# A hybrid decoder step: five page buffers instead of four, nineteen operand buffers instead of eighteen, and a quarter of the dynamic DMA scratch

## The chip, the cores and the metric

The kernel runs on one core of one Trainium2 chip. The metric is the device time of one execution in microseconds (us), as the median of several runs. All data and all results are 32-bit floats.

## What is computed

The reference is one inference step of a decoder layer (DEPTH 1) for two groups of rows that share the weights: a prompt of 1024 rows of width 1024, and 8 sample rows, each with a paged cache of 8192 past positions (64 pages of 128 positions, 8 heads of 64, looked up through a page table). Cut to what matters:

```python
def fox_attend(q, k, v, cq, ck, qpos, kpos):
    s = jnp.einsum('bqhd,bkhd->bhqk', q, k) * (ATT_HEAD_DIM ** -0.5)
    s = s + (cq.transpose(0, 2, 1)[:, :, :, None] - ck.transpose(0, 2, 1)[:, :, None, :])
    s = jnp.where(kpos[None, :] <= qpos[:, None], s, -jnp.inf)
    p = jax.nn.softmax(s, axis=-1)
    return jnp.einsum('bhqk,bkhd->bqhd', p, v)

# the prompt; the samples do the same with k, v, logf of the cache in front of their own
q, k, v, logf, u, z = mixer_inputs(rmsnorm(xp, g_mix), w_in, b_f, g_sgu_v)
xp = xp + merge_heads(fox_prompt(q, k, v, logf), sgu_prompt(u, z, w_s, b_s), g_att_out, g_sgu_out, w_o)
mk, mv = memory_kv(mem_prompt, g_mem, w_ck, w_cv)             # 256 memory rows, 4 heads of 256
xp = xp + cross_attend(rmsnorm(xp, g_cross), mk, mv, w_cq, w_co)
f, conv_p = conv_ffn(rmsnorm(xp, g_ffn), 0, w_up, conv_w, conv_b, w_down)   # width 2 x 2816, silu gate
xp = xp + f
y_prompt = rmsnorm(xp, g_final)
```

`cq` and `ck` are the running sums of the log forget gates. Besides both groups' outputs the new keys, values, gates and states are returned.

## The kernel before

Two streams of work are emitted together. The **main stream** is the prompt, in two halves of 512 rows: projections, attention with spatial gating beside it, the output projection, cross-attention, the gated feed-forward and the final norm. Each large product is made on TensorE (PE) from three matmuls (`gemm3`, L272 to L274) of weights and operands that ScalarE (ACT, L235) and VectorE (DVE, L236, L239) split into a high and a low part. Weight blocks are loaded on SP's queue into `wr`; operands lie in tiles of 128 x 1024, called `u`.

The **sample stream** is the generator `decode`, and after it `sample_rest`. For each of the 8 samples it takes 16 K pages and 16 V pages, each of 128 x 2048 floats, one step at a time. `kstep` (L1428) gathers a K page into a `kv` tile by an indirect DMA that GpSimd (POOL) issues; DVE multiplies it in place with the query and sums over each head into the scores `s` (L1444 and L1448, or in four quarter steps L1435 and L1436 while the main stream is in its attention). `vstep` (L1489) gathers a V page likewise, and 16 narrow matmuls on PE (L1495) add its share to `dv`. Two pages of K and two of V alternate in the order of allocation. After `decode`, the same tiles carry the samples' weights (L1568), and at the start of the kernel they carry the prompt's rows and the sample rows.

In the attention, PE makes a block of scores (L807 to L811), DVE its row maximum (`mx`, L813 and L816), ACT the exponentials (L814, L817); PE turns these (L836), ACT or DVE copies them (L841, L843), and PE multiplies them with V (L852). In the output projections a row factor `fac` is made by ACT (L1031) and a power on POOL (L1032). In the cross-attention ACT copies the turned weights (L1208) before the product at L1216.

A table `PACE` sets how often the sample stream takes a step beside the main stream. This sets the order in which the instructions are written; the page's DVE and PE work is pinned behind the newest instruction of the main stream on that engine (`behind`). Then the framework's scheduler sorts each engine's instructions anew, by its own model of times in which buffers that are in use hold work back. So the number of buffers changes the order on every engine.

The tiles come from rotating pools. A new tile takes the oldest buffer of its kind and waits until that buffer's last reader is done:

```python
def U(shape, dt=F32):
    ...
    t = upool.tile([P, UW], dt, tag="u", bufs=NU, name=nm("u"))[:, :n]
    ...
def KV():
    return dpool.tile([P, 2048], F32, tag="kv", bufs=NKV, name=nm("kv"))
```

Constants lie in on-chip memory behind a scratch area that the program reserves for the dynamic DMAs of GpSimd, by default 16384 bytes on each partition; the pools follow.

Of the kernel before, what the change touches and what calls it, by code (L numbers as in the profile page):

```python
# [47 lines left out]

NKV = 4
VLAG = 2
MIXR = 1.0
G0R = 0.0
# [9 lines left out]
M3 = 3  # L64
MB = 0
BR = 3
NU = 18
NT = 7
HP = 1
SD = 1  # L70
# [8 lines left out]
def build(nc, tc, ctx, a, phases=None):  # L79
# [27 lines left out]
    def nm(s):  # L107
        cnt[0] += 1
        return f"{s}_{cnt[0]}"

    def U(shape, dt=F32):
        n = 1
        for s in shape[1:]:
            n *= s
        t = upool.tile([P, UW], dt, tag="u", bufs=NU, name=nm("u"))[:, :n]
        if len(shape) == 3:
# [6 lines left out]
    def KV():  # L123
        return dpool.tile([P, 2048], F32, tag="kv", bufs=NKV, name=nm("kv"))

# [1909 lines left out]
```

## Time and profile before

| what | us |
|---|---|
| runs | 1790.96, 1792.46, 1794.57 |
| median | 1792.46 |
| profiled execution, span (the page gives no other time of its own) | 1791.7 |
| PE busy | 1735.9 |
| DVE busy | 1399.9 |
| ACT busy | 733.5 |
| POOL busy | 488.3 |

The profile shows one execution. PE, DVE, ACT and POOL are the engines named above, PEld the loading of weights into PE, SP the queue that issues most plain DMAs. A row such as `kv<-cache_k,io` names the tile written and the tensors read; `dv` and `s` are the sample attention's sums and scores. A wait `A x L1 <- B y L2` means that engine A stood before line L1 until B's work at L2 was done. A bracket behind a row is the engine's idle time before it and what ended it. The stages lie, in us from the span's start, roughly so: projections to 315, attention 315 to 500 (the rest of it and the gating after that), first output projection and cross-attention to 715, first feed-forward to 1110, the second half's merge from there, its output projection and cross-attention 1170 to 1345, its feed-forward and the samples' rest to 1779, and the last norm.

### The profile page before, as it was taken

What the parts mean: (1) busy time and instruction counts of PE and PEld (TensorE: products, weight loads), DVE (VectorE), ACT (ScalarE), POOL (GpSimd) and SP (SyncE); (2) the same over time, 40 slices, a digit from 0 to 9 for tenths busy, and PEclk for the clock granted to TensorE, in tenths of its full rate; (3) what the DMA queues carried; (4) which work ended last, traced back from release to release, by engine and by line L of the source; (5) the groups of instructions that cost most, each with busy time, mean ns of one, the idle gap of its engine ahead of it and who ended that gap; (6) DMA issues with size and microseconds to landing.
All of it is one profiled execution on the core that took longest, in us unless ns stands there. A gap on an engine that the chain in (4) does not pass through costs nothing.

```text
span 1791.7 us, 25124 instructions
## 1 busy us (share of the span) xinstructions
PE 1735.9 (97%) x9653; PEld 1285.7 (72%) x9653; DVE 1399.9 (78%) x1733; ACT 733.5 (41%) x1374; POOL 488.3 (27%) x461
## 2 busy tenths in 40 slices
PE   8999999889999999999999999999999999999997
PEld 5787777655677666767777777766666778768875
DVE  4689658989788986989999999898885549855344
ACT  6332355566643635333333244335353233333232
POOL 1252234443222332333322223433322112102110
PEclk9999999999999999999999999999999999999999
DMA  8786798777697975779788788988879587568982
GB/s 291 297 304 226 294 334 319 259 264 244 254 403 279 363 299 224 282 285 345 290 301 313 291 317 311 376 306 346 320 280 350 214 306 249 191 260 297 359 310 80
DMA packets 157074, 521.06 MB, mean 291 GB/s; under 512 B 20874, under 2 KB 40842, under 8 KB 124186
## 3 DMA queue, kind: packets, MB, share of 16 engines
q0 software_dynamic: 57168, 341.14, 50.0%
q1 hardware_dynamic: 92874, 165.73, 26.5%
q10 hardware_dynamic: 6912, 12.59, 1.9%
q8 instruction: 76, 1.25, 0.3%
q14 instruction: 44, 0.36, 0.1%
HBM read 495.47 MB, written 23.93 MB: 290 GB/s over the span
## 4 chain that ended last, share of the span: by engine, by line
PE 53%; issue 9%; DMA 8%; DVE 6%; ACT 2%; POOL 2%; POOLq 0%; DVEq 0%; ACTq 0%; SPq 0%
DMA kv<-cache_v,io 6%; PE ba L272 6%; PE ba L274 6%; PE ba L273 6%; PE dv L1495 4%; PE bb L272 3%; PE bb L273 3%; PE bb L274 3%; PE ba L1063 1%; DVE s L1448 1%; PE ba L1064 1%; PE ba L1065 1%; PE dv L331 1%; DMA kv<-cache_k,io 1%; PE dv L1774 1%
## 5 line engine op out<-in xcount | busy, mean ns | idle before, releaser
L235 ACT ACTIVATE wh<-wr 128x1024 fp32r<-128x1024 f32 (+2 forms) x220 | 228.6, 1044 | 443.3 <-PE ba L273 142.3
L236 DVE TENSOR_TENSOR wl<-wr,wh 128x1024 fp32r<-128x1024 f32 (+2 forms) x220 | 262.7, 1200 | 165.1 <-PE ba L274 57.4
L1428 POOL DMA_INDIRECT kv<-cache_k,io x128 | 186.9, 1460 | 606.8 <-DVE s L1448 327.2
L1444 DVE TENSOR_TENSOR kv<-kv,d 128x1024 f32<-128x1024 f32 (+1 forms) x156 | 258.0, 1681 | 32.6 <-DMA kv<-cache_k,io 32.6
L1448 DVE TENSOR_REDUCE s<-kv 128x16 f32<-128x1024 f32 (+1 forms) x156 | 258.4, 1672 | 0.0
L1489 POOL DMA_INDIRECT kv<-cache_v,io x128 | 160.8, 1256 | 239.4 <-PE dv L1495 155.2
L272 PE MATMUL ba<-u,wh 128*128 128x512 f32 x528 | 209.3, 397 | 0.0
L274 PE MATMUL ba<-u,wl 128*128 128x512 f32 x528 | 209.0, 396 | 0.0
L273 PE MATMUL ba<-u,wh 128*128 128x512 f32 x528 | 208.5, 395 | 0.5 <-DVE u L239 0.5
L272 PE MATMUL ba<-wh,u 128*128 128x512 f32 (+1 forms) x495 | 186.1, 379 | 0.9 <-ACT u L235 0.9
L273 PE MATMUL ba<-wl,u 128*128 128x512 f32 (+1 forms) x495 | 185.1, 375 | 1.3 <-DVE wl L236 1.3
L274 PE MATMUL ba<-wh,u 128*128 128x512 f32 (+1 forms) x495 | 183.4, 375 | 0.0
L1495 PE MATMUL dv<-kv,s 128*32 128x512 f32 x1024 | 127.1, 598 | 1.6 <-DMA kv<-cache_v,io 1.6
L274 PEld LDWEIGHTS ba<-u,wl 128*128 128x128 f32 x528 | 99.2, 188 | 29.0 <-issue 6.5
L272 PEld LDWEIGHTS ba<-u,wh 128*128 128x128 f32 x528 | 99.3, 188 | 26.4 <-issue 4.8
L273 PEld LDWEIGHTS ba<-u,wh 128*128 128x128 f32 x528 | 99.2, 188 | 25.2 <-issue 2.3
L272 PEld LDWEIGHTS ba<-wh,u 128*128 128x128 f32 x495 | 93.0, 188 | 25.0 <-issue 6.5
L272 PE MATMUL bb<-u,wh 128*128 128x512 f32 x272 | 108.7, 400 | 0.0
L274 PE MATMUL bb<-u,wl 128*128 128x512 f32 x272 | 108.0, 398 | 0.0
L273 PE MATMUL bb<-u,wh 128*128 128x512 f32 x272 | 107.9, 397 | 0.0
L273 PEld LDWEIGHTS ba<-wl,u 128*128 128x128 f32 x495 | 93.0, 188 | 20.1 <-DVE wl L236 1.9
L274 PEld LDWEIGHTS ba<-wh,u 128*128 128x128 f32 x495 | 92.9, 188 | 19.5 <-issue 1.6
(454 smaller groups left out, 3310.6 us busy)
## 6 DMA issues: line engine op xcount, KB each, us to landing
wr<-w_up SPq DMA_DIRECT2D x88, 512.0 KB
kv<-w_up POOLq DMA_DIRECT2D x22, 1024.0 KB
wr<-w_down SPq DMA_DIRECT2D x40, 512.0 KB
kv<-w_down POOLq DMA_DIRECT2D x11, 1024.0 KB
wr<-w_in SPq DMA_DIRECT2D x16, 512.0 KB
wr<-w_o SPq DMA_DIRECT2D x16, 512.0 KB
wr<-w_cq SPq DMA_DIRECT2D x16, 512.0 KB
wr<-w_co SPq DMA_DIRECT2D x16, 512.0 KB
```

Source lines behind the costliest of these rows:

```text
L235: nc.scalar.activation(h, src, AF.Copy)
L236: nc.vector.tensor_tensor(l, src, h.bitcast(F32), op=ALU.subtract)
L272: mmul(out, sh, mh, start=(i == 0), stop=False)
L273: mmul(out, sh, ml, start=False, stop=False)
L274: mmul(out, sl, mh, start=False, stop=(i == n - 1))
L331: mmul(ps[32 * j : 32 * j + 32, :w], xT[:, k, :] if nk == 8 else xT[:, k * 8 : k * 8 + 32], raw[:, q, j * w : (j + 1) * w], start=(k == 0) ...
L1063: mmul(pss[i], mh[k][:, tb], wh, start=(k == korder[0]), stop=False)
L1428: nc.gpsimd.indirect_dma_start(kv, None, a["cache_k"], off(kidx[:, b, ch : ch + 1]))
L1444: nc.vector.tensor_tensor(kvv[:, i : i + m, :], kvv[:, i : i + m, :], qb.unsqueeze(1).broadcast_to((P, m, 512)), op=ALU.mult)
L1448: nc.vector.tensor_reduce(s[:, ch * 4 + i : ch * 4 + i + m, :].rearrange("p k h -> p (k h)"), kvv[:, i : i + m, :].rearrange("p k (h d) -> ...
L1489: nc.gpsimd.indirect_dma_start(kv, None, a["cache_v"], off(kidx[:, b, ch : ch + 1]))
L1495: mmul(dv[32 * j : 32 * j + 32, :], s[:, ch * 4 : ch * 4 + 4, :].rearrange("p k h -> p (k h)"), kvv[:, j, :], start=(ch == 1), stop=(ch == ...
```

## The change

Three numbers change. The dynamic scratch takes 4096 bytes on each partition instead of 16384, which frees 12,288. A fifth `kv` buffer takes 8192 of these and a nineteenth `u` buffer 4096.

```diff
-NKV = 4
+NKV = 5
...
-NU = 18
+NU = 19
...
-    nc = bacc.Bacc("TRN2", target_bir_lowering=False, num_devices=1)
+    nc = bacc.Bacc("TRN2", target_bir_lowering=False, num_devices=1, dynamic_dma_scratch_size=4096)
```

No instruction is added or removed on any engine; the order changes. Lines of difference between the orders before and after: PE 3002, DVE 1300, ACT 746, POOL 300, SP 168.

The first place is POOL's queue in the first feed-forward, about 750 to 780 us in the profile. The rows are page gathers; `kv_6843` and `kv_6844` are the V pages that the matmuls at 782 us read. In brackets stand the semaphores that a gather waits for (DMASW for an earlier page's landing, DVE or PE for the last reader of the buffer). Before:

```order
L1428 DMA kv_6751<-cache_k,io 128x2048 [waits DMASW6_49,DVE_49]
L1428 DMA kv_6839<-cache_k,io 128x2048 [waits DMASW7_49,DVE_49]
L1489 DMA kv_6844<-cache_v,io 128x2048 [waits DMASW2_49,PE_49]
L1489 DMA kv_6843<-cache_v,io 128x2048 [waits DMASW0_49,PE_49]
L1428 DMA kv_6883<-cache_k,io 128x2048 [waits DMASW3_49,DVE_49]
L1428 DMA kv_6973<-cache_k,io 128x2048 [waits DMASW6_49,PE_49]
```

The same six gathers after the change:

```order
L1428 DMA kv_6751<-cache_k,io 128x2048 [waits DMASW3_49,DVE_49]
L1428 DMA kv_6839<-cache_k,io 128x2048 [waits DMASW6_49,DVE_49]
L1489 DMA kv_6844<-cache_v,io 128x2048 [waits DMASW7_49,DVE_49]
L1489 DMA kv_6843<-cache_v,io 128x2048 [waits DMASW3_49,DVE_49]
L1428 DMA kv_6883<-cache_k,io 128x2048 [waits DMASW1_49,PE_49]
L1428 DMA kv_6973<-cache_k,io 128x2048 [waits DMASW0_49,PE_49]
```

The gathers keep their order here; what moved is the buffer that each one takes. The two V pages took the buffers of two earlier V pages, which PE reads, and now take those of K pages, which DVE reads.

The second place is DVE's order in the attention's second half. `d` is the query of a sample, L1435 and L1436 are quarter steps of a K page, `mx` a row maximum, `rl` and `u` belong to the main stream.

```order
 L1435 TENSOR_TENSOR kv_3757<-kv_3757,d_490_2860 128x512
 L863 RECIPROCAL rl_3957<-ls_3732 128x4
+L1435 TENSOR_TENSOR kv_3917<-kv_3917,d_490_2860 128x512
+L1436 TENSOR_REDUCE s_2862<-kv_3757 128x8
+L816 TENSOR_REDUCE mx_3896<-ba_3897 128x1
+L1436 TENSOR_REDUCE s_2862<-kv_3757 128x8
 L816 TENSOR_REDUCE mx_3933<-ba_3934 128x1
-L1436 TENSOR_REDUCE s_2862<-kv_3757 128x8
-L1435 TENSOR_TENSOR kv_3917<-kv_3917,d_490_2860 128x512
-L816 TENSOR_REDUCE mx_3973<-ba_3974 128x1
-L1436 TENSOR_REDUCE s_2862<-kv_3757 128x8
 L1436 TENSOR_REDUCE s_2862<-kv_3917 128x8
```

A product and two sums of pages that stood behind the maximum `mx_3933` stand ahead of it now, and `mx_3896`, made earlier before, stands among them. Over the whole attention 48 such quarter rows stood directly ahead of a maximum before, and 59 after.

The third place is POOL's queue around the row factors of the output projection that ends the second half's cross-attention, about 1316 us. `fac_2060`, `fac_2070`, `fac_2074` are three of its four factors, the other rows are V pages.

```order
 L1489 DMA kv_10835<-cache_v,io 128x2048
+L1489 DMA kv_10985<-cache_v,io 128x2048
+L1489 DMA kv_10984<-cache_v,io 128x2048
 L1032 TENSOR_TENSOR fac_2060_10931<-fac_2060_10931,mhalf 128x1
-L1489 DMA kv_10985<-cache_v,io 128x2048
+L1489 DMA kv_11203<-cache_v,io 128x2048
 L1032 TENSOR_TENSOR fac_2070_11012<-fac_2070_11012,mhalf 128x1
-L1489 DMA kv_10984<-cache_v,io 128x2048
-L1489 DMA kv_11203<-cache_v,io 128x2048
 L1489 DMA kv_11204<-cache_v,io 128x2048
+L1489 DMA kv_11253<-cache_v,io 128x2048
 L1032 TENSOR_TENSOR fac_2074_11023<-fac_2074_11023,mhalf 128x1
```

Two pages moved ahead of the first factor and a third, `kv_11203`, ahead of the second.

## The prediction

> **What bounds the kernel now.** I read the page's engine shares first, then the busy times in stretches, then the waits of all engines, then the timelines of the few PE rows that wait for work made from cache pages.
>
> ```profile
> span 1791.7 us, 25124 instructions
> PE 1735.9 (97%) x9653; PEld 1285.7 (72%) x9653; DVE 1399.9 (78%) x1733; ACT 733.5 (41%) x1374; POOL 488.3 (27%) x461
> ...
> q0 software_dynamic: 57168, 341.14, 50.0%
> ```
>
> PE is busy for 1735.9 of 1791.7 us, so no edit that leaves its matmuls alone can gain more than the 55.8 us in which it is idle, plus what the clock takes. The stretches tell where those 55.8 lie (stretch, length, busy time of PE, PEld, DVE, ACT, POOL, granted clock, DMA share, GB/s):
>
> ```profile
> 0.00:30.00 30.00, 22.85 (x92) 14.74 (x93) 16.38 (x45) 16.31 (x23) 0.98 (x6) 1.00 0.72 235
> 30.00:60.00 30.00, 29.57 (x143) 22.84 (x142) 4.92 (x10) 14.93 (x26) 10.15 (x10) 1.00 0.99 397
> 60.00:75.00 15.00, 12.57 (x103) 11.25 (x98) 12.11 (x7) 9.29 (x13) 0.00 (x0) 1.00 0.78 278
> 315.00:500.00 185.00, 165.27 (x1109) 115.66 (x1109) 162.26 (x287) 113.04 (x251) 63.60 (x82) 0.96 0.76 260
> 575.00:715.00 140.00, 134.43 (x669) 96.60 (x671) 114.64 (x144) 66.46 (x156) 40.24 (x35) 0.99 0.78 304
> 715.00:1110.00 395.00, 393.69 (x1859) 293.49 (x1852) 372.04 (x344) 141.91 (x220) 113.70 (x82) 1.00 0.81 302
> 1170.00:1345.00 175.00, 167.22 (x868) 117.83 (x867) 151.01 (x181) 78.83 (x174) 58.16 (x50) 1.00 0.83 313
> 1779.00:1792.00 13.00, 3.40 (x15) 2.44 (x13) 5.68 (x10) 1.45 (x4) 1.58 (x3) 0.73 0.40 161
> ```
>
> Length less PE busy gives 10.0 us in the first 75 us, 19.7 in the attention (315 to 500), 5.6 and 7.8 in the two middles (output projection and cross-attention), 1.3 in the whole first feed-forward, 9.6 behind the last matmuls. The attention is the only long stretch with a granted clock clearly below 1. There, as at 699.6, the rate falls to half for stretches of 3.4 us; the stretches at 317.3, 354.8, 368.5 (two in a row) and 699.6 make 17.0 us at half rate, of which these are the first and the last:
>
> ```profile
> 317.30:320.70 3.40, 2.98 (x16) 2.27 (x16) 3.31 (x6) 0.62 (x3) 0.60 (x1) 0.50 1.05 408
> ...
> 699.60:703.00 3.40, 3.40 (x18) 3.40 (x17) 2.27 (x7) 0.58 (x2) 1.01 (x1) 0.50 0.64 266
> ```
>
> One such stretch with PE busy costs about half of 3.4, 1.7 us.
>
> Now the page buffers. The waits of all engines (total, times, longest):
>
> ```profile
> POOL kv L1428 <- DVE s L1448: 327.2, 68, 28.2
> POOL kv L1489 <- PE dv L1495: 155.2, 41, 11.4
> POOL kv L1428 <- PE dv L1495: 127.5, 18, 14.7
> ...
> DVE kv L1444 <- DMA kv<-cache_k,io: 32.6, 18, 5.6
> ```
>
> POOL issues the page gathers and waits over 600 us for one of the four buffers. That is idle time of an engine with 27% work and costs nothing by itself. What counts is whether DVE (for K) and PE (for V) meet a page that has not landed. DVE does so 18 times, 32.6 us in all. On PE I followed every idle gap back to its releaser; these five end at a page (start, length, row, idle before):
>
> ```profile
> 626.71 1.92 PE L1495 MATMUL dv<-kv,s 128*32 128x512 f32 x16 [0.33 <-DMA kv<-cache_v,io]
> 633.71 1.12 PE L1216 MATMUL ba<-u,t 128*128 128x512 f32 x2 [0.58 <-ACT u L1209]
> 782.27 1.92 PE L1495 MATMUL dv<-kv,s 128*32 128x512 f32 x16 [1.31 <-DMA kv<-cache_v,io]
> 1111.92 0.65 PE L943 MATMUL bb<-cp,u 128*128 128x128 f32 x4 [0.79 <-DVE u L239]
> 1259.55 1.13 PE L1216 MATMUL ba<-u,t 128*128 128x512 f32 x2 [1.03 <-ACT u L1209]
> ```
>
> Two wait for a V page directly; the one at 633.71 waits for ACT work released behind the late matmuls of 626.71; the last two have on DVE, ahead of what they need, a row that waits for a K page:
>
> ```profile
> 1105.52 2.29 DVE L1444 TENSOR_TENSOR kv<-kv,d 128x2048 f32<-128x2048 f32 x1 [1.42 <-DMA kv<-cache_k,io]
> ...
> 1247.42 2.36 DVE L1444 TENSOR_TENSOR kv<-kv,d 128x1024 f32<-128x1024 f32 x2 [0.90 <-DMA kv<-cache_k,io]
> ```
>
> The five sum to 0.33 + 0.58 + 1.31 + 0.79 + 1.03 = 4.0 us. That is all that late pages cost PE in this execution.
>
> **The change part by part.** The profile gives no time for the execution beside its span, 1791.7; the median of the runs, 1792.46, is 0.8 above it. I apply the sum to both.
>
> *The fifth page buffer.* No instruction is added or removed; every page takes a buffer whose last reader is one page further back, so its gather can be issued earlier. By the rows of POOL's waits a gather stands 327.2/68 = 4.8 us for a K buffer and 155.2/41 = 3.8 for a V buffer, and with a spare buffer it can go about that much sooner (an estimate; the order held fixed). A page lands 10.2 us after its issue, by the chain's rows
>
> ```profile
> 772.02 10.21 DMA kv<-cache_v,io
> ...
> 1237.66 9.73 DMA kv<-cache_k,io
> ```
>
> and the longest lateness on DVE is 5.6, on PE 1.31. An advance of 3.8 to 4.8 therefore covers nearly all of them: −4.0 us on PE's path (bounds −4.0 and 0). The rest of DVE's waits, 32.6 − 1.42 − 0.90 = 30.3 us, goes too, but PE hardly feels it: I price it at PE's idle share in the second middle, where half of them lie, 7.78/175 = 4.4%, so −1.3 (bounds 0 and all of that middle's idle time, −7.8). What is late next is the operand that PE waits for in the middles, made by DVE and ACT from PE's own results.
>
> *The new order.* The scheduler sorts each engine's rows anew, with pages thought to come earlier. In the attention a page's products and sums are cut into quarters:
>
> ```profile
> L1435 DVE TENSOR_TENSOR kv<-kv,d 128x512 f32<-128x512 f32 x64 | 43.1, 693 | 0.1
> L1436 DVE TENSOR_REDUCE s<-kv 128x8 f32<-128x512 f32 x64 | 41.7, 675 | 0.1
> L816 DVE TENSOR_REDUCE mx<-ba 128x1 f32<-128x640 f32 (+3 forms) x32 | 32.3, 1016 | 7.8 <-PE ba L811 7.6
> L813 DVE TENSOR_REDUCE mx<-ba 128x1 f32<-128x128 f32 (+3 forms) x32 | 15.4, 484 | 0.8 <-PE ba L811 0.2
> ```
>
> Counted in DVE's order, 48 of these quarter rows stand directly ahead of a score maximum (L813 or L816) before, 59 after. PE needs the maximum for the exponentials, the transposes and the next scores. Eleven more rows of 0.68 us are 7.5 us of later maxima; at PE's idle share in that stage, 19.7/185 = 11%, +0.8 (bounds 0, the delay being covered by the other score blocks, and +7.5). Below nothing is possible as well, since other maxima move forward.
>
> *POOL's order.* Around the row factors of the output projection that ends the second half's cross-attention, two V pages more are queued ahead of the second factor:
>
> ```profile
> 1316.39 1.43 POOL L1032 TENSOR_TENSOR fac<-fac,mhalf 128x1 f32<-128x1 f32 x1 [1.69 <-ACT fac L1031]
> ...
> 1321.08 1.72 POOL L1489 DMA_INDIRECT kv<-cache_v,io  x1 [3.25 <-DVE s L1448]
> ```
>
> The page that started at 1321.08 waits for a DVE sum; if it starts as before, the factor behind it starts at 1321.08 + 1.72 = 1322.8 instead of 1316.39, 6.4 us later. With a buffer more it is released by an earlier sum, so I take 0 and keep +6.4.
>
> *The head.* The first page waits for the load of the sample rows' tile, the fifth for a DVE sum:
>
> ```profile
> 36.35 1.17 POOL L1428 DMA_INDIRECT kv<-cache_k,io  x1 [22.49 <-DMA kv<-x]
> 79.05 0.95 POOL L1428 DMA_INDIRECT kv<-cache_k,io  x1 [28.18 <-DVE s L1448]
> ```
>
> After the change the first can go in the stretch 0 to 30, where DMA is at 0.72, and the fifth joins in 30 to 60, where it is at 0.99 and 397 GB/s. A page is 128 × 2048 × 4 bytes = 1.05 MB, 2.6 us at that rate; one leaves the full stretch and one enters it: 0 (bounds −2.4, PE's idle time in 60 to 75, and +2.6). [...]
>
> *The operand buffer and the scratch.* The nineteenth operand tile lets ACT and DVE prepare one more operand tile ahead. No row of PE's waits names an operand buffer, so 0 (bound below: half of the middles' idle time, in the rivals). The smaller scratch costs 0: with 57168 packets and 341.14/1.05 = 325 pages' worth of data, a page is 57168/16/325 = 11 packets on each DMA engine, and five pages 55. [...]
>
> Sum: −4.0 − 1.3 + 0.8 = −4.5 us. The span would be 1787.2, the median 1792.46 − 4.5 = 1788.0. A difference of 0.2% is 3.6 us, about what a measurement of this kernel can tell from no change.
>
> **The rivals.**
>
> *More comes out of the middles.* The extra operand tile and earlier pages halve their idle time: (5.57 + 7.78)/2 = 6.7, and the half-rate stretch at 699.6 disappears, 1.7: 1784.0. For it: these are the stages where DVE meets late pages. Against: PE there mostly waits for short chains on DVE and ACT. With the waits of the sum that lie outside the middles, about 2 us, it would be 1782.
>
> *The waits move on.* Each of the five gaps is filled by the next wait, as DVE is 86% busy in the middle and 88% in the attention: 1792. For it: none is longer than 1.31 us.
>
> *The early fifth page delays the first weight loads*: −4.5 + 2.6 = −1.9, 1790.6. Against: the first page leaves the full stretch.
>
> *The maxima come later, slower.* One mechanism: in the attention DVE does page quarters where it did maxima. All eleven rows reach PE, +7.5; two of PE's longer waits there bring another half-rate stretch each, +3.4; less the 4.0: +6.9, 1799.4. It decides when eight of the eleven rows reach PE (8 × 0.68 is the whole gain of 5.3). For it: DVE is busy for 162.26 of 185 us there, PE waits for exponentials behind these maxima, and the clock has already dropped four times. Without any gain from pages it is 7.5 + 3.4 = +10.9, 1803.
>
> *POOL's queue holds the second factor*: +6.4, another half-rate stretch 1.7, less 5.3: +2.8, 1795.3.
>
> [...]
>
> **How the numbers follow.** Forecast 0.40, its own range 1786 to 1791, of which 0.25 is faster than 1788.9 (0.2%) and 0.15 within; more out of the middles 0.13; waits move on 0.09; head 0.05; later maxima 0.23; POOL's queue 0.08; ring 0.02. Faster: 0.25 + 0.13 = 0.38. Same: 0.15 + 0.09 + 0.05 = 0.29. Slower: 0.23 + 0.08 + 0.02 = 0.33. The cases of both signs hold much of the chance, so the range goes from 1780, a little below the larger gain, to 1803, later maxima without a gain.
>
> **What would show it.** Right: the five gaps on PE gone or below 0.3 us, DVE's wait for K pages under 10 us, POOL's waits for DVE's sums shorter, PE's idle time in 315 to 500 within 2 us of 19.7, the clock there still 0.96. Later maxima: that idle time above 25 us and more half-rate stretches. POOL's queue: the second row factor of that projection later than the PE rows around it, with a PE gap of several us near 1320. Head: more PE idle time than 2.43 us in 60 to 75. [...] The forecast is wrong if the attention stage moves by more than the pages' 4 us in either direction.

## The result: 1811.2 us instead of 1791.7, and the profile after

The median is 1811.22 us (four runs, 1808.93 to 1814.01) against 1791.71 (1790.88 to 1794.57; the three runs of the table above and a fourth): a ratio of 1.0093, 95% interval 1.0069 to 1.0117. The forecast was 1788.0 with a range of 1780 to 1803. The profiled execution's span is 1807.1, 15.4 above the one of before. Its page:

```profile
span 1807.1 us, 25125 instructions
PE 1745.3 (97%) x9653; PEld 1290.0 (71%) x9653; DVE 1398.8 (77%) x1733; ACT 733.5 (41%) x1374; POOL 479.4 (27%) x461
```

The busy times in stretches of the changed kernel (columns as in the prediction):

```profile
30.00:60.00 30.00, 29.95 (x139) 22.83 (x137) 5.12 (x10) 15.92 (x27) 9.96 (x10) 1.00 1.01 407
60.00:75.00 15.00, 12.72 (x97) 10.73 (x98) 8.61 (x7) 9.27 (x12) 0.00 (x0) 1.00 0.86 282
75.00:315.00 240.00, 236.67 (x1259) 184.54 (x1259) 193.58 (x189) 93.02 (x157) 82.73 (x71) 0.99 0.77 284
315.00:500.00 185.00, 161.62 (x1113) 111.08 (x1109) 158.59 (x284) 111.01 (x255) 60.00 (x81) 0.98 0.78 267
500.00:575.00 75.00, 70.65 (x343) 55.92 (x344) 65.73 (x86) 26.23 (x51) 19.25 (x14) 0.93 0.82 306
715.00:1110.00 395.00, 394.15 (x1868) 295.98 (x1868) 369.01 (x350) 141.58 (x223) 109.96 (x82) 1.00 0.79 297
1170.00:1345.00 175.00, 169.67 (x860) 119.89 (x852) 154.50 (x181) 81.28 (x173) 62.96 (x48) 1.00 0.87 330
```

The same view of the kernel before for two stretches that the prediction did not look at:

```profile
75.00:315.00 240.00, 239.62 (x1285) 186.75 (x1283) 192.25 (x194) 97.26 (x170) 86.31 (x71) 1.00 0.80 291
500.00:575.00 75.00, 75.00 (x398) 58.89 (x397) 66.34 (x88) 28.79 (x51) 21.74 (x16) 1.00 0.88 330
```

PE was never idle in 500 to 575 and hardly so in 75 to 315; it now idles 4.4 and 3.3 us there, and runs part of both at half rate. Stretches of the clock cut across stages, so I also took PE's lost time between landmarks of the main stream: from the trace's matmul rows, the time from one start to the next beyond the lower quartile of its kind, summed.

```
lost on PE, us                              before  changed
start to the first scores (L807)              27.7     35.8
attention (to its last L872)                  77.9     74.9
to the first output projection's last L1063    0.2      7.1
to its last L1081                              1.8      1.8
to the last L280 behind the norm               1.7      7.7
cross-attention, feed-forward (to L943)       37.5     34.8
the ten other stretches together             126.4    126.3
```

The loss sits in three places: 8.1 us in the projections, 6.9 at the attention's end, 6.0 at the norm in front of the cross-attention. The attention gains 3.0, and the stretch from that norm to the last L943 2.7. The sizes depend on what is counted as a kind: counted in other ways, the three losses come out at 6 to 9, 6 to 8 and 5 to 6 us, and the attention's gain at 1 to 4. Plain time between the same landmarks (starts of their rows), in which moved sample work counts too, gives 5.7, 7.3 and 6.5 us for the losses and 1.6 and 2.7 for the gains.

The attention's gain is not shown to be the change's. The profile of e1 below, whose order and buffers are those of before, has the attention 2.9 us shorter, with one half-rate stretch in it where before has four.

Of the three losses some is the clock: before the last norm the changed kernel has eight half-rate stretches of 3.4 us, three more than before, by estimate 5 us (half of 3.4 for each). (The number varies from one execution to the next: e1 has two.) Four of the eight lie in the three places; these two (rows of the same view) lie right behind the gaps named below:

```profile
170.10:173.50 3.40, 3.40 (x9) 2.66 (x9) 3.40 (x3) 0.24 (x1) 1.72 (x2) 0.50 0.99 386
501.20:504.60 3.40, 3.40 (x10) 2.56 (x10) 3.40 (x6) 3.40 (x8) 0.00 (x0) 0.50 1.07 396
```

**The pages did come earlier.** DVE's row for whole and half pages, with the wait for a landing at its end, was 32.6 us and is now

```profile
L1444 DVE TENSOR_TENSOR kv<-kv,d 128x1024 f32<-128x1024 f32 (+1 forms) x156 | 257.7, 1680 | 11.4 <-DMA kv<-cache_k,io 11.4
```

**The first place, the projections.** Besides the wait at the start, which the kernel before has too, PE's longest waits are new ones (two rows of its waits):

```profile
PE ba L273 <- DVE wl L236: 3.9, 4, 2.9
PE ba L1063 <- ACT u L238: 3.6, 1, 3.6
```

The first is at 169.36. DVE's timeline of the changed kernel there, and below it that of the kernel before:

```profile
154.91 8.88 DVE L1444 TENSOR_TENSOR kv<-kv,d 128x2048 f32<-128x2048 f32 x4
163.71 4.46 DVE L1448 TENSOR_REDUCE s<-kv 128x32 f32<-128x2048 f32 x2
168.10 1.20 DVE L236 TENSOR_TENSOR wl<-wr,wh 128x1024 fp32r<-128x1024 f32 x1
```

```profile
151.75 6.68 DVE L1444 TENSOR_TENSOR kv<-kv,d 128x2048 f32<-128x2048 f32 x3
158.35 2.27 DVE L1448 TENSOR_REDUCE s<-kv 128x32 f32<-128x2048 f32 x1
160.55 2.27 DVE L1444 TENSOR_TENSOR kv<-kv,d 128x2048 f32<-128x2048 f32 x1
162.75 1.21 DVE L236 TENSOR_TENSOR wl<-wr,wh 128x1024 fp32r<-128x1024 f32 x1
```

Six whole-page rows now run ahead of the weight's low part that PE needs, where five did: one sum of 2.2 us more. And the run of them starts 3.2 us later. So L236 starts 5.35 us later than before, at a place that PE reaches 1.3 us later. Of the other 4 us about 1.1 was slack before, by PE's rows there, and 2.9 is what PE waits.

**The second place, the attention's end.** PE, POOL and ACT of the changed kernel, in this order:

```profile
486.19 1.07 PE L1495 MATMUL dv<-kv,s 128*32 128x512 f32 x8 [1.26 <-DMA kv<-cache_v,io]
487.77 1.06 PE L1495 MATMUL dv<-kv,s 128*32 128x512 f32 x8
...
500.68 0.50 PE L1063 MATMUL ba<-wh,u 128*128 128x512 f32 x1 [3.61 <-ACT u L238]
```

```profile
487.56 1.03 POOL L1489 DMA_INDIRECT kv<-cache_v,io  x1 [5.66 <-PE dv L1495]
489.14 0.94 POOL L1489 DMA_INDIRECT kv<-cache_v,io  x1 [0.56 <-PE dv L1495]
```

```profile
493.31 1.06 ACT L235 ACTIVATE wh<-wr 128x1024 fp32r<-128x1024 f32 x1 [4.26 <-DMA wr<-w_o]
495.75 0.38 ACT L861 ACTIVATE t<-bb 128x256 f32<-128x256 f32 x1 [1.38 <-PE bb L852]
498.99 1.06 ACT L235 ACTIVATE wh<-wr 128x1024 fp32r<-128x1024 f32 x1 [2.85 <-DMA wr<-w_o]
499.95 1.25 ACT L238 ACTIVATE u<-bb,gp 128x512 fp32r<-128x512 f32 x2
```

And PE and ACT before:

```profile
488.70 1.92 PE L1495 MATMUL dv<-kv,s 128*32 128x512 f32 x16
```

```profile
488.80 0.69 ACT L238 ACTIVATE u<-bb,gp 128x512 fp32r<-128x512 f32 x1 [0.20 <-PE bb L943]
490.13 1.06 ACT L235 ACTIVATE wh<-wr 128x1024 fp32r<-128x1024 f32 x1 [0.64 <-DMA wr<-w_o]
```

Read as a chain: the sixteen V matmuls (eight for each of two pages and not sixteen, as 1024 rows for 128 pages show) stand earlier among PE's rows; as they end they free two page buffers; POOL sends two V pages at 487.6 and 489.1, where before it sent none between 478.76 and 490.06; a load of `w_o` lands behind them; ACT stands before its split for 2.85 us with the operand split (L238) behind it; PE waits 3.61 for that. This load is in the chain of work (start, us from issue to landing):

```profile
484.53 14.44 DMA wr<-w_o
```

By the landings in the traces its counterpart before, the third load of `w_o`, took 9.1 us. The wait of 4.26 is of another sort: the second load lands 10.4 us after its issue, against 9.4 before, and ACT stands before it for long because L235 now comes ahead of L238. Whether it is really such a chain the runs below decide.

### The profile page after: what moved, and what is told of

Same layout as the page of the kernel before. It is cut to its first block, busy times and chain, and to the rows that moved or that the text cites. A ratio compares the mean times of both kernels' runs of the same rounds, so it can differ in the third digit from the quotient of the medians.

```text
span 1807.1 us, 25125 instructions
## 1 busy us (share of the span) xinstructions
PE 1745.3 (97%) x9653; PEld 1290.0 (71%) x9653; DVE 1398.8 (77%) x1733; ACT 733.5 (41%) x1374; POOL 479.4 (27%) x461
## 4 chain that ended last, share of the span: by engine, by line
PE 68%; DVE 3%; ACT 1%; DMA 1%; issue 1%; POOL 0%; DVEq 0%; POOLq 0%; ACTq 0%; SPq 0%
PE ba L272 10%; PE ba L273 10%; PE ba L274 10%; PE dv L1495 5%; PE bb L272 5%; PE bb L274 5%; PE bb L273 5%; PE ba L1063 1%; PE ba L1064 1%; PE dv L331 1%; PE ba L1065 1%; PE dv L1774 1%; DMA wr<-w_o 1%; PE ba L1082 1%; PE ba L1081 1%; PE ba L1083 1%
## 5 line engine op out<-in xcount | busy, mean ns | idle before, releaser
L235 ACT ACTIVATE wh<-wr 128x1024 fp32r<-128x1024 f32 (+2 forms) x220 | 228.6, 1043 | 444.8 <-PE ba L273 126.1
L236 DVE TENSOR_TENSOR wl<-wr,wh 128x1024 fp32r<-128x1024 f32 (+2 forms) x220 | 262.5, 1199 | 159.0 <-PE ba L274 49.9
L1489 POOL DMA_INDIRECT kv<-cache_v,io x128 | 174.0, 1359 | 453.0 <-PE dv L1495 275.8
L1428 POOL DMA_INDIRECT kv<-cache_k,io x128 | 165.4, 1293 | 379.8 <-DVE s L1448 249.6
```

Of the source, the lines that this page charges most:

```text
L235: nc.scalar.activation(h, src, AF.Copy)
L236: nc.vector.tensor_tensor(l, src, h.bitcast(F32), op=ALU.subtract)
L1428: nc.gpsimd.indirect_dma_start(kv, None, a["cache_k"], off(kidx[:, b, ch : ch + 1]))
L1489: nc.gpsimd.indirect_dma_start(kv, None, a["cache_v"], off(kidx[:, b, ch : ch + 1]))
```

## The experiments

Three theories stood at first: the new **order** on the engines costs the time; the **traffic** of a fifth page does, whatever the order; the smaller scratch (theory **ring**) does. The first four runs set the parts of the change apart. Each set of runs has its own runs of the kernel before beside it, with medians from 1792.56 to 1795.17, so the ratios are the numbers to compare.

**e1, the scratch alone.** `NKV = 4`, `NU = 18`, `dynamic_dma_scratch_size=4096`.

> Scratch of 4096 alone, four page and eighteen operand buffers; the order on every engine is that of the kernel before. Theory 'order' (the new order on the engines costs the time), theory 'traffic' (the earlier pages load the DMA engines and weights come late) and theory 'operand' all expect 1791.7, within 0.2% of before. Theory 'ring' (a quarter of the scratch holds POOL's gathers up) expects most of the 19.5 us: above 1805.

Ratio 0.9995 (0.9979 to 1.0012). Theory 'ring' is out.

**e2, the page buffer alone.** `NKV = 5`, `NU = 18`, `dynamic_dma_scratch_size=8192`.

> Five page buffers alone, scratch 8192, eighteen operand buffers. PE's and SP's orders are those of the changed kernel, DVE's, ACT's and POOL's differ from it in 16, 13 and 8 lines. Theories 'order' and 'traffic' expect the changed kernel's 1811 (1806 to 1814). Theory 'operand' expects under 1796, theory 'ring' under 1796 if 8192 is enough.

1809.6, ratio 1.0079 (1.0052 to 1.0105): the page buffer carries the loss.

**e3, the operand buffer alone.** `NKV = 4`, `NU = 19`, `dynamic_dma_scratch_size=12288`.

> Nineteen operand buffers alone, scratch 12288, four page buffers. The order differs from before in 150 lines on PE, 78 on DVE. Theory 'operand' expects above 1805; the three others expect 1791.7, within 0.4%.

Ratio 1.0020 (1.0002 to 1.0039). At most a small part.

**e4, the old order.** The program is built twice: once as before, to read each engine's order, and once with the change, where order-only edges make each engine follow that list. They add no wait. In outline:

```diff
+    order = order_of(program(4, 18, 16384))
+    nc = program(5, 19, 4096, order)
...
+                if e in last:
+                    tc.add_manual_dep(here[name], last[e], NoSync)
+                last[e] = name
```

> The whole change (five page buffers, nineteen operand buffers, scratch 4096), but every engine, the transfers' queues too, follows instruction for instruction the order that the kernel before has. Theory 'order' expects the loss gone, and the gain that the prediction counted for pages, 4 us: 1786 to 1792. Theory 'traffic' expects the pages, which are free to go earlier by one buffer, to press on the weights: above 1800. Theory 'ring' expects above 1805.

1798.4, ratio 1.0021 (1.0007 to 1.0036), between what two of the theories expected. Most of the loss goes with the order, but the expected gain does not come. Its trace says why. POOL there, and below it POOL before at the same place:

```profile
290.74 1.03 POOL L1428 DMA_INDIRECT kv<-cache_k,io  x1 [0.30 <-PE ba L811]
292.07 0.96 POOL L1428 DMA_INDIRECT kv<-cache_k,io  x1 [0.30 <-issue]
293.34 0.94 POOL L1489 DMA_INDIRECT kv<-cache_v,io  x1 [0.30 <-issue]
```

```profile
290.06 1.58 POOL L1428 DMA_INDIRECT kv<-cache_k,io  x1 [2.57 <-DVE mx L813]
291.94 0.97 POOL L1428 DMA_INDIRECT kv<-cache_k,io  x1 [0.30 <-DVE wl L236]
...
299.39 1.38 POOL L1489 DMA_INDIRECT kv<-cache_v,io  x1 [6.48 <-PE dv L1495]
```

The fifth buffer lets a third page go out at 293, just ahead of four loads of `w_cv` that SP issues from 294.7. By the landings in the traces the first of these loads takes 10.4 us behind the three pages; before, it was issued at 290.8 behind one page and took 3.8. ACT and PE of e4 (timeline, and a row of PE's waits):

```profile
305.12 1.06 ACT L235 ACTIVATE wh<-wr 128x1024 fp32r<-128x1024 f32 x1 [6.44 <-DMA wr<-w_cv]
```

```profile
PE ba L807 <- ACT t L814: 6.9, 2, 6.7
```

The attention lost 87.9 us there instead of 77.9, with 20.5 us at half rate. So traffic looks like a cause too, in another place; e8 tests it.

**e5 and e6, the old order in one stage alone**, the rest sorted anew (same edges, only between instructions of that stage).

> The changed kernel, but the instructions of the projections follow the order of the kernel before on every engine; the rest is sorted anew. Theory 'order' says that the changed kernel loses there because DVE does four whole-page steps in a row ahead of a weight's low part (a PE gap of 2.9 us at 169 and a half-rate stretch behind it), 5.7 us up to the first scores: 1805 to 1808 here against the changed kernel's 1811. Theory 'traffic' says that the pages alone do it: 1811.

1804.5, ratio 1.0058 (1.0043 to 1.0074). The projections lose 29.6 us instead of 35.8; behind the attention it loses 8.6 and 6.3 us, where the changed kernel loses 7.1 and 7.7.

> The changed kernel, but the instructions of the first half's output projection and cross-attention follow the order of the kernel before. The changed kernel loses 13 us between the end of the attention and the norm of the cross-attention. Theory 'order' expects most of that back: 1797 to 1803. Theory 'traffic' (the loads of w_o land late, since more pages are under way) expects at least the 7 us at the attention's end to stay: 1804 to 1811.

1795.0, ratio 1.0007 (0.9992 to 1.0022), better than expected. The stretches behind the attention lose 0.2 and 1.7, as before; the projections still 36.9. So the order in this one stage is worth nearly as much as the whole net loss. The projections' loss stays, and shorter stretches elsewhere (by the landmarks 2.8 us in the attention, 2.5 behind the norm) make up for most of it.

**e7, the computing engines in the old order, POOL and SP free.** The edges of e4 for PE, DVE and ACT only.

> The whole change, PE, DVE and ACT in the order of the kernel before, POOL and SP sorted anew, so that pages may go ahead of POOL's other work and weight loads in another order. Theory 'order' expects the time of the run with all five orders old, 1798 (1795 to 1801). If the places of the page gathers in POOL's queue matter by themselves, it is above 1801.

1788.2, ratio 0.9969 (0.9954 to 0.9984): faster than both kernels, and by 0.5% faster than e4. The scheduler, which now sees the buffers that are there, sends a K and a V page at that place and holds the third back:

```profile
291.47 1.59 POOL L1428 DMA_INDIRECT kv<-cache_k,io  x1 [2.62 <-DVE mx L813]
293.36 0.97 POOL L1489 DMA_INDIRECT kv<-cache_v,io  x1 [0.30 <-DVE wl L236]
```

DVE's wait for K pages is down from 32.6 to

```profile
L1444 DVE TENSOR_TENSOR kv<-kv,d 128x1024 f32<-128x1024 f32 (+1 forms) x156 | 257.9, 1680 | 1.5 <-DMA kv<-cache_k,io 1.5
```

and PE has no wait for a page at all. I had expected no difference from e4; the queues' order matters as much as the fifth buffer's gain. By the landmarks e7 is 2.7 us shorter than before from the norm to the last L943 and 3.1 behind that; the first half's output projection takes the time of before, and the attention is as short as in e1.

**e8, the old order with the pages held back.** e4 and, up to the attention's end, a wait of each gather for the last reader of the page four gathers before. In outline:

```diff
+        for old, gather in zip(fills, fills[4:]):
+            if gather in early stages:
+                tc.add_manual_dep(gather, last_reader[old], Sync)
```

> The whole change with all orders old, as in the earlier run at 1798, and in the projections and the attention each page gather also waits, as with four buffers, for the last reader of the page four gathers before it; from the first output projection on the fifth buffer is free. Theory 'traffic' (in the run with old orders a third page under way held the loads of w_cv, ACT stood 6.4 us before one of them, PE 6.9, and the clock fell) expects that gap gone and the gain of the first feed-forward, 2.5 us, kept: 1786 to 1791 where before is 1791.7, a ratio of 0.996 to 1.000. If the loss has another cause, it stays at 1.002.

1790.8, ratio 0.9980 (0.9961 to 0.9998). The gap at 300 is gone, the first load of `w_cv` takes 3.5 us again, and the attention loses 75.5. So in e4 the cause was the pages that went out early, ahead of these loads.

**e9 to e12, one engine at a time in the stage of e6.**

> The changed kernel, with ACT alone following the old order in the first half's output projection and cross-attention; the other engines are sorted anew around it. In the changed kernel the split of a w_o block (L235) stands on ACT ahead of the last operand split of the attention (L238), and waits there for its load. If that place on ACT makes the gap at the attention's end, those 7 us are gone and the 6 us at the norm stay: 1802 to 1806. If both gaps hang on ACT: 1797 to 1800. If neither: 1811.

> The same with DVE alone. If DVE's order makes the gaps at the norm (there PE waits for the residual sums and splits that stand on DVE behind weight splits and gating rows), those 6 us go: 1803 to 1807; if the gap at the attention's end also hangs on it: 1797 to 1800; if neither: 1811.

> The same with PE alone. In the changed kernel a group of V matmuls (L1495) stands ahead of the attention's last rows; it frees two buffers, two V pages go out at 487 and 489 us, and the w_o loads land behind them. If that is the origin of the gap at the attention's end, it goes here too: 1802 to 1806, or 1797 to 1800 with the gap at the norm; else 1811.

> The same with POOL and SP alone, the two that issue the transfers. If the queues' order of pages and w_o loads makes the gap at the attention's end: 1802 to 1806. If the order on the computing engines does: 1811, unchanged.

ACT: 1808.2, 1.0078 (1.0048 to 1.0108); the gap at the attention's end stays (6.2 lost), the one at the norm shrinks to 3.7. DVE: 1812.1, 1.0095 (1.0064 to 1.0127). POOL and SP: 1811.6, 1.0102 (1.0073 to 1.0130). PE: 1804.4, 1.0055 (1.0038 to 1.0071), with both gaps closed (0.2 and 1.6 lost) and a new one opened in the cross-attention, at 570 us (PE's waits):

```profile
PE ms L1481 <- DVE dg L1474: 4.2, 1, 4.2
```

Here PE's old order meets a DVE that is sorted anew. The profiled execution of this run is its fastest (1797.2); what the others, up to 1805.2, lose beside it is not shown. The start of both gaps is on PE; the place of ACT's weight split, which I would have named from the trace, is a link and not the start.

**e13, one group of V matmuls.** The changed kernel, with the matmuls on the two pages `kv_4666` and `kv_4667` queued behind the row of L943 behind which they stood before. In outline:

```diff
+        for i in V_matmuls_of(kv_4666, kv_4667):
+            tc.add_manual_dep(i, last_row_writing(bb_4646), NoSync)
```

> The changed kernel with one edit: the matmuls of one V page pair (L1495 on kv_4666 and kv_4667), which in the changed kernel stand among the attention's last turns, are pinned behind the last rows of L943 that write bb_4646, where the kernel before has them; all else is sorted anew. If these matmuls start the gap at the attention's end (they wait for a page, free two buffers there, and the w_o loads fall behind two more pages), the 7 us go and the time is 1800 to 1805; if the sorting behind them also mends the gap at the norm, 1796 to 1800. If they are a symptom only: 1809 to 1812.

1797.4, ratio 1.0023 (1.0009 to 1.0037) against the changed kernel's 1.0093: 0.7% or some 12 us for sixteen matmuls that last 1.9 us. PE, POOL and ACT of this run:

```profile
490.99 1.92 PE L1495 MATMUL dv<-kv,s 128*32 128x512 f32 x16
...
493.26 0.48 PE L1063 MATMUL ba<-wh,u 128*128 128x512 f32 x1
```

```profile
492.36 0.94 POOL L1489 DMA_INDIRECT kv<-cache_v,io  x1 [10.18 <-PE dv L1495]
```

```profile
491.10 0.69 ACT L238 ACTIVATE u<-bb,gp 128x512 fp32r<-128x512 f32 x1 [0.20 <-PE bb L943]
492.72 1.06 ACT L235 ACTIVATE wh<-wr 128x1024 fp32r<-128x1024 f32 x1 [0.93 <-DMA wr<-w_o]
```

The pages go out at 492 instead of 487.6, and the stretches lose 1.6 and 2.5 instead of 7.1 and 7.7. The edit also let the scheduler put ACT's L238 back ahead of L235, which is why ACT waits 0.93 for the second load of `w_o` instead of 4.26; so by its time alone e13 does not part traffic from ACT's order. Two things do. In e9, where ACT's order alone was old, the gap stays. And the third load of `w_o`, issued at nearly the same moment (484.5 and 484.6), lands 14.4 us after its issue in the changed kernel and 8.0 us after it in e13. All traces agree: where two V pages go out 1.7 to 4.6 us behind the issue of this load (the changed kernel, e2, e5, e9, e10, e12, e14), it takes 14.2 to 14.5 us; in the ten other traces the next page goes out 7.7 us behind it or later, and it takes 8.0 to 9.5. So here too the early pages hold the load up.

**e14, DVE alone in the projections.**

> The changed kernel with DVE alone in the old order during the projections. If DVE's four whole-page steps ahead of a weight's low part make the loss there, it gives what the old order of all engines in the projections gave, 1804 to 1806; if the loss there comes from the other engines, 1811.

1805.5, ratio 1.0068 (1.0049 to 1.0087): as much as all engines gave in e5, though the interval touches the changed kernel's. In its trace the gap at 169 and the half-rate stretch behind it are gone, and the first scores come 4.6 us earlier. The first place is DVE's order.

**e15, e7 without the nineteenth operand buffer**: `NU = 18`, scratch 8192.

> PE, DVE and ACT in the old order and POOL and SP sorted anew, as in the run at 0.997 of before, but with eighteen operand buffers and a scratch of 8192: five page buffers alone. If the gain is the pages', the ratio is again 0.995 to 0.998; if the nineteenth operand buffer has a part in it, 0.999 to 1.002.

1788.9, ratio 0.9972 (0.9958 to 0.9985), the same as e7 within the intervals. The gain needs no nineteenth operand buffer; it is the pages'.

## Why the prediction was wrong

*The pages' term, −4.0 and −1.3: right in mechanism, and about right in size, the latter in part by luck.* In the changed kernel the gaps at 626, 782 and 1111 are gone, and the stretch to the last L943 gains 2.7 us; a new late page appears at 486. With the computing engines' order held (e7, e15) the whole is 0.3%, 5 to 6 us, against my 5.3. But two of the five gaps were not, or not wholly, a page's: in e7, where PE waits for no page, the rows of 633.71 and 1259.55 both still wait 0.58 us (0.32 and 1.50 in the changed kernel). So late pages cost PE 2.9 us in these gaps, not 4.0.

*The term "the new order", +0.8 with bounds 0 and 7.5: the step that failed.* I priced the new order on the computing engines in one stage and by one pattern, the page quarters ahead of score maxima. That stage did not lose: 77.9 us before, 74.9 now, a difference within what two executions of one order show. The order's cost lay in two places that I did not price at all, since nothing waited there before: DVE's page rows ahead of a weight split in the projections (e5, e14), and one group of V matmuls on PE at the attention's end (e6, e13). The profile of before showed 0.38 us of idle time in 75 to 315 and none in 500 to 575, and I took such a stretch for safe. It means only that the order of before hid everything there. The difference of PE's order held the moved V matmuls for anyone to see; I had counted PE's lines of difference (3002) and not asked what each moved group frees or delays. So the upper bound was a bound of one pattern, not of the order, and the range ended 8 us too low.

*"What is late next" was answered wrongly.* I named operands made by DVE and ACT. It was the weight loads that the earlier pages push back: `w_o` in the changed kernel, `w_cv` in e4. I did put a rival of this kind at the head of the kernel, at 0.05 and +2.6; between 30 and 75 PE's idle time went from 2.86 to 2.33, so there it did nothing in the changed kernel. (In e4, e5 and e7, with the old order there, the first scores came 1.4 to 2.5 us later than before, behind one half-rate stretch at 63; one execution each, so a small cost at the head stays possible.) The mechanism was right and the place wrong. It decided in e4, where a third page met loads that ACT splits next, and there it cost PE a wait of 6.7 us and half-rate stretches behind it, not 2.6, since ACT stood with the exponentials behind the split. That the pages hold these loads up, e4 and e8 show, though not by what way: in e4 ACT waits 6.44 us for a load of SP's queue behind pages of POOL's, in e8, with the pages held back, 0.4 us in all for these loads.

*The rivals.* Later maxima: 0.23 for the right sign by the wrong mechanism; of it only the half-rate stretches came true, three more. POOL's queue: the second factor there now started at 1326.64 and waited only for ACT, and the projection lost 7.2 instead of 6.6, without any idle time of PE there; refuted. The waits move on (1792): one new page wait came, at 486, but the gaps that cost the time were not filled-up page gaps. More out of the middles: refuted, since the first one lost. A loss by the smaller scratch ("ring" among the chances): refuted by e1, and with five pages by e7 and e15, which agree at scratches of 4096 and 8192. That a page's packets bear on the size of the scratch, on which its term of 0 rested, no run shows; with the scratch alone e1 came to a ratio of 0.9995. The operand buffer at 0: right within 0.2% (e3, e15).

*Still open:* why the gap at the norm (6.0 us) follows the one at the attention's end. PE's old order closes it and DVE's alone does not; ACT's leaves 2.0 of the 6.0 us. That it is the same delay carried on is argued, not shown. Open too is what makes e11 slower than its profiled execution.

## What to carry to other kernels

Where a scheduler sorts the work by the buffers it has, one more buffer is two changes, and they can be measured apart by replaying the old order with the new buffers; here the buffer was worth −0.3% with the transfers sorted anew (e7; +0.2% with their old order, e4), and the order that it brought on the computing engines +1.2% (1.0093/0.9969). A stretch without idle time is not a stretch without risk: for each group that moves ahead on the bound engine, ask which buffers it frees, which transfers that lets go, and which loads an engine is about to wait for with needed work behind the wait (here 2.85 us on ACT, with L238 behind it). Hold the order on the computing engines and let the scheduler sort the transfers alone: here that beat both kernels.

## What the runs showed of the hardware

In the changed kernel the clock fell to half for 3.4 us also at a gap much shorter than that. The last of the eight stretches starts at 1347.7, near the end of a gap of 1.65 us on PE (a row of its timeline in the changed kernel, and the stretch):

```profile
1347.91 0.48 PE L1124 MATMUL bb<-cp,u 128*128 128x128 f32 x1 [1.65 <-DVE u L1045]
```

```profile
1347.70:1351.10 3.40, 3.19 (x15) 3.19 (x16) 1.72 (x5) 1.64 (x5) 0.00 (x0) 0.50 0.00 0
```

In the 3.40 us ahead of it (1344.30 to 1347.70) PE was busy for 1.79 us, at a granted clock of 1.00. The other two drops named above stand behind longer gaps: the one at 170.1 behind 2.9 us, with PE busy for 0.74 of the 3.40 us ahead, and the one at 501.2 behind 3.61 us, with 0.52. What decides whether a gap brings a drop is not settled here.
